# Five edits to a mixer-and-MLP layer: the causal mask as a select, the gate weight moved from v to k, a convolution tap and the first norm's squares on ScalarE, and a broadcast load issued earlier

## The chip, the cores and the metric

The kernel runs on one core of one Trainium2 chip. The metric is the device time of one execution in microseconds (us). The kernel before took 1031.86, 1032.71 and 1033.84 us in three runs (median 1032.71). All arithmetic is on float32 data; most matrix products split each float32 operand into a rounded high part and a remainder and add three products of the parts.

## The reference, cut to what matters

One layer over 1024 tokens (rows) of 1024 channels. The steps that the change touches are these:

```
u = x @ w_in                                   # q, k, v, gates, output gate, pooling columns
qk = silu(causal_conv(u[q,k columns], w_conv)) # 4 taps: y[t] = sum_j w[j] * u[t - 3 + j]
# mLSTM, 4 heads x 128, chunk by chunk, with exponential input gate e and decay
C_loc = einsum(e, v, k);  n_loc = einsum(e, k) # state update of a chunk, weighted by e
C = s_old * C + s_new * C_loc
Dlog = where(causal, a_t - a_s + i_s, -inf)    # decay inside a chunk
P = exp(Dlog - m_t);  qk = (q k^T) * P         # masked weights
h = (qk @ v + s_inter * (C q)) / denominator   # then a norm per head and an output gate
mix = concat(h, pooled) @ w_out
x1 = layer_norm(2**0.25 * x + mix, ln1_g, ln1_b)
out = layer_norm(2**0.25 * x1 + square(relu(x1 @ w_ff1)) @ w_ff2, ln2_g, ln2_b)
```

## The kernel before

**Stages.** The tokens are worked on in two halves of 512, each as four tiles of 128 rows. Calls near line 990 lay out the order: projections of the first half (output gate, pooling, v and gates, q, k), then those of the second half with the first half's mLSTM chunks mixed in, then the output projection with the second half's chunks mixed in, and then the MLP. The mLSTM works in chunks of 128 rows, four chunks in each half. The MLP is computed as products over blocks of 512 with seven instead of eight block products per group (a Strassen-like scheme), `jobs` in the code: `n` counts the products, and each has its operands made by `prep`, its 192 matrix instructions by `product`, and its results added into buffers by `evict1` or `evict2`.

**How the order is set.** A list `tasks` holds steps that fall due a number of ticks later (`later`, `tick`); a tick comes twice in a group of projection products. `mlstm` hands each chunk's four stages to it, so that a chunk's small products lie between the large ones. Beyond that the compiler's planner orders each engine's queue: it takes instructions in program order as their inputs come free by its own estimates of their durations, and adds the waits. Each engine and each DMA-issuing queue then runs strictly in that order; an instruction that waits holds back all behind it. `after(...)` keeps one instruction behind another in that plan.

**A chunk** (`mlstm_stages`, line 554). Its decay rows come by SP from a DRAM bounce buffer to `ng` (broadcast over 128 partitions, 128x512) and, but for the first chunk, `si`. GpSimd adds the tile `mask` (0 or -1e30) to `ng` (line 564); ScalarE takes four exponentials with a per-row bias (line 566). TensorE forms q k (line 571) into a bank of the pool `ps_ml`, VectorE multiplies it into `ng` (line 572), GpSimd multiplies q into `si` (line 574). TensorE transposes k (line 578) into a bank of `ps_tr`, ScalarE copies it out as `kt` (line 580), and GpSimd makes `vs`, v times the gate weight `ep` (line 582). Two products give the chunk's output (lines 591, 592), one the state update (line 599, into a bank of `ps_tr`), which VectorE folds into the state `C` (line 605). Lines 608 to 624 are the norm per head on VectorE: many instructions on 4 columns, each on the one before. `ps_ml` and `ps_tr` have two banks each, so a product waits for the engine that empties the bank two uses earlier. The pooling group's map uses `ps_ml` too (line 437); ScalarE and VectorE empty it (lines 440, 441).

**The convolution** (`proj_qk`, line 377) runs on 16 blocks of 128 channels: ScalarE copies a block's product to `u` behind three carried columns (line 393), VectorE forms the first tap (line 397) and adds three more (line 399), ScalarE applies SiLU.

**The first norm** (`out_proj`, line 670): for each pair of row tiles VectorE adds the scaled x to the product (line 697) and takes statistics of each 512 columns (line 698); after the second column half they are joined (line 701), `ln_rsqrt` uses ScalarE for the root, and ScalarE scales and shifts the rows (line 710). The transposes of line 730 need the result.

**The residual** (`residual`, line 862): its first call loads `ln1_g` to all partitions through GpSimd's DMA queue into `lngb` (line 866); its four later calls multiply it into the rows (VectorE, line 870) and add `ln1_b` by an accumulating DMA (line 871). The loop calls it after products 2 to 6. The same queue carries stores of the token operands (line 852) and the accumulating loads that sum weight blocks (line 815).

Of the kernel before, what the change touches and what calls it, by code (L numbers as in the profile page):

```python
# [9 lines left out]
F32 = mybir.dt.float32  # L10
# [5 lines left out]
P = 128  # L16
# [6 lines left out]
def trunk_layer(ctx: ExitStack, tc: tile.TileContext, x, w_in, b_gate, w_conv, hn_g,  # L23
# [36 lines left out]
    def big(shape, dt=F32, name="b"):  # L60
        return bigp.tile(shape, dt, tag="big", name=nm(name))

    def sml(shape, tag, bufs=2):
        return small.tile(shape, F32, tag=tag, name=nm(tag), bufs=bufs)
# [49 lines left out]
    def tick(n=1):  # L114
        for _ in range(n):
            clock[0] += 1
            while True:
                due = [t for t in tasks if t is not None and t[0] <= clock[0]]
                if not due:
# [12 lines left out]
    tri = const.tile([P, P], F32, name="tri")  # L132
    pool.memset(tri, 1.0)
    pool.affine_select(out=tri, in_=tri, pattern=[[1, P]], compare_op=ALU.is_ge, fill=0.0,
                       base=0, channel_multiplier=-1)
    mask = const.tile([P, P], F32, name="mask")
    pool.memset(mask, 0.0)
    pool.affine_select(out=mask, in_=mask, pattern=[[1, P]], compare_op=ALU.is_ge, fill=NEG,
                       base=0, channel_multiplier=-1)
    rcnt = const.tile([P, 16], F32, name="rcnt")  # L140
    for t in range(16):
# [235 lines left out]
    def proj_qk(hf, which, w=None):  # L377
        w = w or wcols(w_in, (OQ, OK)[which], 512)
        dst = (qT, kT)[which]
        for j in range(TT):  # L380
            c = hf * TT + j
            if hf == 0:
                dst[c] = big([P, 4, P], name="qk")
            else:
                if which == 1:
                    qT["pair", c] = zp.tile([P, 2, 4, P], F32, tag="z", name=nm("qk"))
                dst[c] = qT["pair", c][:, which]
        for cp in (0, 2):
            for cb, ps in zip((cp, cp + 1), chan_mm(hf, w, (cp, cp + 1))):
                b = 4 * which + cb  # L390
                u = big([P, HT + 3], name="u")
                dve.tensor_copy(u[:, 0:3], qkc[:, b, :])
                act.copy(u[:, 3:], ps)
                if hf == 0:
                    dve.tensor_copy(qkc[:, b, :], u[:, HT:HT + 3])
                a = big([P, HT], name="cv")
                dve.tensor_scalar(a, u[:, 0:HT], pcol[:, b:b + 1], None, op0=ALU.mult)
                for j in range(1, 4):
                    dve.scalar_tensor_tensor(a, u[:, j:j + HT], pcol[:, 8 * j + b:8 * j + b + 1], a,
                                             op0=ALU.mult, op1=ALU.add)  # L400
                for j in range(TT):
                    act.activation(dst[hf * TT + j][:, cb, :], a[:, j * P:(j + 1) * P], AF.Silu)
            tick()
        return w
# [149 lines left out]
    def mlstm_stages(c):  # L554
        hf, j = divmod(c, TT)
        g = G[hf]
        last = c == S // P - 1
        ng = big([P, 4, P], name="ng")
        si = big([P, 4, P], name="si") if c else None
        for i, t in ((0, ng), (1, si))[:2 if c else 1]:  # L560
            src = g["dr"][i, 4 * j:4 * j + 4, :]
            sp.dma_start(t.rearrange("p h t -> p (h t)"),
                         src.rearrange("h t -> (h t)").unsqueeze(0).to_broadcast([P, 512]))
        pool.tensor_tensor(ng, ng, mask.unsqueeze(1).to_broadcast([P, 4, P]), ALU.add)
        for h in range(4):
            act.activation(ng[:, h, :], ng[:, h, :], AF.Exp, bias=g["b"][:, 1, 4 * j + h:4 * j + h + 1])
        yield
        q, k, v = qT[c], kT[c], v1[c]
        ps = mlps([P, 4, P])
        for h in range(4):  # L570
            pe.matmul(ps[:, h, :], lhsT=k[:, h, :], rhs=q[:, h, :], start=True, stop=True)
        dve.tensor_tensor(ng, ng, ps, ALU.mult)
        if c:
            pool.tensor_tensor(si, si, q, ALU.mult)
        if not last:
            pk = trps([P, 4, P])
            for h in range(4):
                pe.transpose(pk[:, h, :], k[:, h, :], ident)
            kt = big([P, 4, P], name="kt")
            act.copy(kt, pk)  # L580
            vs = big([P, 4, 129], name="vs")
            pool.tensor_tensor(vs, v, g["ep"][:, 4 * j:4 * j + 4].unsqueeze(2).to_broadcast([P, 4, 129]),
                               ALU.mult)
        yield
        o = big([P, 4, 129], name="o")
        for hp in range(2):
            po = mlps([P, 2, 129])
            for i in range(2):
                h = 2 * hp + i
                if c:  # L590
                    pe.matmul(po[:, i, :], lhsT=si[:, h, :], rhs=C[:, h, :], start=True, stop=False)
                pe.matmul(po[:, i, :], lhsT=ng[:, h, :], rhs=v[:, h, :], start=(c == 0), stop=True)
            act.copy(o[:, 2 * hp:2 * hp + 2, :], po)
        if not last:
            for hp in range(2):
                pcl = trps([P, 2, 129])
                for i in range(2):
                    h = 2 * hp + i
                    pe.matmul(pcl[:, i, :], lhsT=kt[:, h, :], rhs=vs[:, h, :], start=True, stop=True)
                if c == 0:  # L600
                    dve.tensor_copy(C[:, 2 * hp:2 * hp + 2, :], pcl)
                else:
                    for i in range(2):
                        h = 2 * hp + i
                        dve.scalar_tensor_tensor(C[:, h, :], C[:, h, :],
                                                 g["so"][:, 4 * j + h:4 * j + h + 1], pcl[:, i, :],
                                                 op0=ALU.mult, op1=ALU.add)
        r, st, mv, w = sml([P, 4], "n_r"), sml([P, 4, 6], "n_st"), sml([P, 4, 2], "n_mv"), sml([P, 4], "n_w")
        den = o[:, :, 128]
        dve.scalar_tensor_tensor(r, den, -1.0, den, op0=ALU.mult, op1=ALU.max)  # L610
        dve.tensor_tensor(r, r, g["thr"][:, 4 * j:4 * j + 4], ALU.max)
        dve.reciprocal(r, r)
        for h in range(4):
# [12 lines left out]
        pt = trps([P, 4, P])  # L626
        for h in range(4):
            pe.transpose(pt[:, h, :], y[:, h, :], ident)
        yh, yl = big([P, 4, P], F32R, "ymh"), big([P, 4, P], F32R, "yml")
        split(yh, yl, pt)  # L630
        yTm[c] = (yh, yl)
# [38 lines left out]
    def out_proj(hf, e, gs=None):  # L670
        w = wo[e]
        for cp in (hf * TT, hf * TT + 2):
# [14 lines left out]
            if e == 0:  # L687
                ln1[cp] = (small.tile([P, 2, 2, 6], F32, tag="l1_st", name=nm("l1_st"), bufs=4),
                           sml([P, 2, 2], "l1_mv"))
            st, mv = ln1[cp]  # L690
            for i, ps in enumerate(pss):
                c = cp + i
                if e == 0:
                    zt[c] = zp.tile([P, 2, 512], F32, tag="z", name=nm("z"))
                    for d in range(2):
                        z[c, d] = zt[c][:, d, :]
                dve.scalar_tensor_tensor(z[c, e], xr[:, i, :], ALPHA, ps, op0=ALU.mult, op1=ALU.add)
                dve.bn_stats(st[:, i, e, :], z[c, e])
            if e == 1:
                for i in range(2):  # L700
                    dve.bn_aggr(mv[:, i, :], st[:, i])
                r = ln_rsqrt(mv[:, :, 1], 2)
                for i in range(2):
                    zs, rs = zt[cp + i], r[:, i:i + 1]
                    if hf == 1 and cp % TT == 2 and i == 1:
                        dve.tensor_scalar(zs, zs, mv[:, i, 0:1], rs, op0=ALU.subtract, op1=ALU.mult)
                        continue
                    shift = sml([P, 1], "l_sh", 4)
                    dve.scalar_tensor_tensor(shift, mv[:, i, 0:1], -1.0, rs, op0=ALU.mult, op1=ALU.mult)
                    act.activation(zs, zs, AF.Identity, scale=rs, bias=shift)  # L710
                    if hf == 0:
                        for d in range(2):
# [309 lines left out]
    for n, (r, ph, i) in enumerate(jobs):  # L1022
# [28 lines left out]
        ends.append(anchor[0])  # L1051
        if ph == 0:
            evict1(i, ps)
            if 2 <= n <= 6:
                residual(n - 2)
        else:
            evict2(i, ps, r)

# [24 lines left out]
```

## Time and profile before

| what | value |
| --- | --- |
| three runs | 1031.86, 1032.71, 1033.84 us |
| the profiled execution | 1032.68 us, of which the span from first to last instruction is 1031.0 us |
| mean granted TensorE clock | 0.993 |
| busy: TensorE matmul, VectorE, ScalarE, GpSimd | 1007.0, 728.5, 453.5, 160.6 us |

The profile page of one execution gives, for each engine, the time in which it was busy; further views group its instructions by code line, list the waits, or show stretches of time. In a row of instructions `out<-in` are the program's names for what is written and read, and a line number is one of the kernel's. PE is TensorE, DVE VectorE, ACT ScalarE, POOL GpSimd, SP the queue that issues most loads. The granted clock (PEclk) is 1.00 at 2.4 GHz and 0.50 at 1.2 GHz.

### The profile page before, as it was taken

The page shows a single profiled execution, that of the slowest core. Times are in us where ns is not written, and L with a number is a line of the kernel's source. Part 1 is how long each engine was busy: PE and PEld are TensorE (multiplying, and loading weights), DVE is VectorE, ACT ScalarE, POOL GpSimd, SP SyncE. Part 2 cuts the span into 40 slices and gives each one's busy share as a digit, 9 for nine tenths or more (in the row PEclk, how much of TensorE's full clock was granted, in tenths as well). Part 3 has the DMA queues.
Part 4 walks back from the last instruction along what each step waited for, and adds up shares of the span by engine and source line. Part 5 has one row for each costly group of instructions (what it writes and reads, how often), then busy time and mean ns, then how long its engine had stood idle before and what let it go on. Part 6 is the DMA issues. An engine that isn't in the chain of part 4 may idle for free.

```text
span 1031.0 us, 12626 instructions
## 1 busy us (share of the span) xinstructions
PE 1007.0 (98%) x4721; PEld 825.6 (80%) x4721; DVE 728.5 (71%) x1199; ACT 453.5 (44%) x649; POOL 160.6 (16%) x199
## 2 busy tenths in 40 slices
PE   9999999999889999999999999999999999999995
PEld 7898789888778887877888888888888888888884
DVE  4664765886988537788875488875488865478877
ACT  4533655648312235443434524434534334534363
POOL 2410002222220103312102002201001302000211
PEclk9999999999989999999999999999999999999998
DMA  8411412423521537997809853809952908902647
GB/s 287 165 62 44 162 43 73 130 75 104 163 62 42 123 129 194 299 290 209 144 2 225 284 183 51 154 1 209 296 178 53 162 1 196 293 1 42 123 92 215
DMA packets 64158, 143.30 MB, mean 139 GB/s; under 512 B 4732, under 2 KB 4832, under 8 KB 64096
## 3 DMA queue, kind: packets, MB, share of 16 engines
q1 hardware_dynamic: 41488, 91.30, 26.5%
q0 software_dynamic: 22368, 50.89, 25.0%
q8 instruction: 37, 0.61, 0.2%
q10 hardware_dynamic: 240, 0.30, 0.1%
q14 instruction: 25, 0.20, 0.1%
HBM read 128.28 MB, written 11.57 MB: 136 GB/s over the span
## 4 chain that ended last, share of the span: by engine, by line
PE 85%; DVE 7%; DMA 3%; issue 2%; ACT 2%; POOL 1%; SPq 0%; DVEq 0%; POOLq 0%; ACTq 0%
PE mm L103 18%; PE mm L104 18%; PE mm L105 18%; PE ml L104 5%; PE ml L103 5%; PE ml L105 5%; PE tr L103 5%; PE tr L104 4%; PE tr L105 4%; DMA w<-in_w_ff_dram 1%; DVE wlo L77 1%; DVE ol L77 1%; PE tr L730 1%; PE tr L174 1%; DMA raw<-in_w_in_dram 1%
## 5 line engine op out<-in xcount | busy, mean ns | idle before, releaser
L77 DVE TENSOR_TENSOR ol<-w,oh 128x1024 fp32r<-128x1024 f32 x112 | 135.8, 1222 | 94.3 <-ACT oh L76 94.1
L76 ACT CAST oh<-w 128x1024 fp32r<-128x1024 f32 x112 | 116.5, 1047 | 152.7 <-PE mm L104 59.0
L103 PE MATMUL mm<-oh,oh 128*128 128x512 f32 x448 | 176.9, 395 | 1.9 <-DVE h L931 1.6
L104 PE MATMUL mm<-ol,oh 128*128 128x512 f32 x448 | 176.7, 394 | 0.9 <-DVE ol L77 0.9
L105 PE MATMUL mm<-oh,ol 128*128 128x512 f32 x448 | 176.3, 394 | 0.0
L815 POOL DMA_DIRECT2D w<-in_w_ff_dram x64 | 76.7, 1281 | 495.3 <-DVE ol L77 473.3
L103 PEld LDWEIGHTS mm<-oh,oh 128*128 128x128 f32 x448 | 84.2, 188 | 22.9 <-ACT oh L76 2.2
L104 PEld LDWEIGHTS mm<-ol,oh 128*128 128x128 f32 x448 | 84.2, 188 | 20.8 <-DVE ol L77 1.3
L105 PEld LDWEIGHTS mm<-oh,ol 128*128 128x128 f32 x448 | 84.2, 188 | 19.8
L104 PE MATMUL ml<-ol,oh 128*128 128x512 f32 x224 | 88.5, 395 | 0.0
L103 PE MATMUL ml<-oh,oh 128*128 128x512 f32 x224 | 88.5, 395 | 0.0
L103 PE MATMUL tr<-oh,oh 128*128 128x512 f32 x224 | 88.3, 394 | 0.0
L105 PE MATMUL ml<-oh,ol 128*128 128x512 f32 x224 | 88.2, 395 | 0.0
L104 PE MATMUL tr<-ol,oh 128*128 128x512 f32 x224 | 88.2, 394 | 0.0
L105 PE MATMUL tr<-oh,ol 128*128 128x512 f32 x224 | 88.1, 393 | 0.0
L77 DVE TENSOR_TENSOR ol<-xs,oh 128x1024 fp32r<-128x1024 f32 x42 | 51.3, 1224 | 47.2 <-ACT oh L76 47.2
L76 ACT CAST oh<-h 128x1024 fp32r<-128x1024 f32 x40 | 41.8, 1048 | 80.3 <-PE ml L104 24.9
L76 ACT CAST oh<-xs 128x1024 fp32r<-128x1024 f32 x42 | 43.9, 1048 | 62.6 <-PE ml L104 38.8
L77 DVE TENSOR_TENSOR wlo<-raw,whi 128x1024 fp32r<-128x1024 f32 (+1 forms) x40 | 51.6, 1299 | 13.6 <-PE mm L105 6.7
L103 PE MATMUL mm<-xT,whi 128*128 128x512 f32 x144 | 57.5, 400 | 0.1
L104 PE MATMUL mm<-xT,whi 128*128 128x512 f32 x144 | 57.0, 396 | 0.0
L105 PE MATMUL mm<-xT,wlo 128*128 128x512 f32 x144 | 56.8, 397 | 0.0
(293 smaller groups left out, 1989.3 us busy)
## 6 DMA issues: line engine op xcount, KB each, us to landing
w<-in_w_ff_dram POOLq DMA_DIRECT2D x64, 512.0 KB, 7.2
w<-in_w_ff_dram SPq DMA_DIRECT2D x58, 512.0 KB, 7.1
xs<-xs SPq DMA_DIRECT2D x42, 512.0 KB, 5.9
raw<-in_w_in_dram SPq DMA_DIRECT2D x27, 512.0 KB, 4.8
xs<-x POOLq DMA_DIRECT2D x12, 512.0 KB, 5.4
raw<-in_w_in_dram SPq DMA_DIRECT2D x8, 520.0 KB, 4.9
raw<-in_w_out_dram SPq DMA_DIRECT2D x8, 512.0 KB, 3.3
xres<-in_x_dram SPq DMA_DIRECT2D x8, 512.0 KB, 3.3
```

The lines of the kernel that those rows point to most:

```text
L76: cast = act.copy(hi, src)
L77: dve.tensor_tensor(lo, src, hi.bitcast(F32), ALU.subtract)
L103: pe.matmul(ps, lhsT=lh, rhs=rh, start=start, stop=False, skip_group_check=grow)
L104: pe.matmul(ps, lhsT=lh, rhs=rl, start=False, stop=False, skip_group_check=grow)
L105: return pe.matmul(ps, lhsT=ll, rhs=rh, start=False, stop=stop, skip_group_check=grow)
L174: pe.transpose(ps[:, a, b, :], raw[:, b, kc * P:(kc + 1) * P], ident)
L730: t0 = pe.transpose(ps[:, j, :], z[hf * TT + j, kb // 4][:, (kb % 4) * P:(kb % 4 + 1) * P], ident)
L815: pool.dma_start(t, w_source(r, ph, q, p), accum_op=ALU.add)
```

## The change

- The tile `mask` is gone. GpSimd sets the entries of `ng` above the diagonal to -1e30 by a select on the index (`affine_select`), in place, instead of an addition.
- `vs` is gone. k is multiplied by the gate weight as its transposed copy is made: four ScalarE instructions with a per-row scale, one a head, instead of one copy; the state update reads v itself.
- The last convolution tap is formed by ScalarE from the product's bank with a per-channel scale; VectorE adds the other three.
- The first norm, but for the last pair of row tiles: the row sums come as a second output of the addition (line 697's instruction), the squares and their sums from four ScalarE instructions after the second column half, and small VectorE instructions make mean and variance of them.
- The first call of `residual`, which loads `lngb`, comes after product 0 instead of product 2. The later calls stay after products 3 to 6.

```diff
-    mask = const.tile([P, P], F32, name="mask")
-    pool.memset(mask, 0.0)
-    pool.affine_select(out=mask, in_=mask, pattern=[[1, P]], compare_op=ALU.is_ge, fill=NEG,
...
-                dve.tensor_scalar(a, u[:, 0:HT], pcol[:, b:b + 1], None, op0=ALU.mult)
-                for j in range(1, 4):
+                act.activation(a, ps, AF.Copy, scale=pcol[:, 24 + b:25 + b])
+                for j in (2, 1, 0):
                     dve.scalar_tensor_tensor(a, u[:, j:j + HT], pcol[:, 8 * j + b:8 * j + b + 1], a,
...
-        pool.tensor_tensor(ng, ng, mask.unsqueeze(1).to_broadcast([P, 4, P]), ALU.add)
+        pool.affine_select(out=ng, in_=ng, pattern=[[0, 4], [1, P]], compare_op=ALU.is_ge, fill=NEG,
+                           base=0, channel_multiplier=-1)
...
-            act.copy(kt, pk)
-            vs = big([P, 4, 129], name="vs")
-            pool.tensor_tensor(vs, v, g["ep"][:, 4 * j:4 * j + 4].unsqueeze(2).to_broadcast([P, 4, 129]),
-                               ALU.mult)
+            for h in range(4):
+                act.activation(kt[:, h, :], pk[:, h, :], AF.Copy, scale=g["ep"][:, 4 * j + h:4 * j + h + 1])
...
-                    pe.matmul(pcl[:, i, :], lhsT=kt[:, h, :], rhs=vs[:, h, :], start=True, stop=True)
+                    pe.matmul(pcl[:, i, :], lhsT=kt[:, h, :], rhs=v[:, h, :], start=True, stop=True)
...
+            last = hf == 1 and cp % TT == 2
...
-                dve.scalar_tensor_tensor(z[c, e], xr[:, i, :], ALPHA, ps, op0=ALU.mult, op1=ALU.add)
-                dve.bn_stats(st[:, i, e, :], z[c, e])
+                if last:
+                    dve.scalar_tensor_tensor(z[c, e], xr[:, i, :], ALPHA, ps, op0=ALU.mult, op1=ALU.add)
+                    dve.bn_stats(st[:, i, e, :], z[c, e])
+                else:
+                    dve.scalar_tensor_tensor(z[c, e], xr[:, i, :], ALPHA, ps, op0=ALU.mult, op1=ALU.add,
+                                             accum_out=st[:, i, e, 0:1])
...
+                    dve.tensor_tensor(neg, st[:, :, 0, 0], st[:, :, 1, 0], ALU.add)
+                    dve.tensor_scalar(neg, neg, -1.0 / 1024, None, op0=ALU.mult)
+                    for i in range(2):
+                        for d in range(2):
+                            act.activation(big([P, 512], name="sq"), z[cp + i, d], AF.Square,
+                                           bias=neg[:, i:i + 1], accum_out=st[:, i, d, 1:2])
+                    dve.tensor_tensor(var, st[:, :, 0, 1], st[:, :, 1, 1], ALU.add)
+                    dve.tensor_scalar(var, var, 1.0 / 1024, None, op0=ALU.mult)
...
-            if 2 <= n <= 6:
-                residual(n - 2)
+            if n == 0 or 3 <= n <= 6:
+                residual(max(n - 2, 0))
```

## Rows read from the trace of the kernel before

**Rows 1.** The page's first part: busy time of TensorE, its share and instructions.

```profile
PE 1007.0 (98%) x4721; PEld 825.6 (80%) x4721; DVE 728.5 (71%) x1199; ACT 453.5 (44%) x649; POOL 160.6 (16%) x199
```

**Rows 2.** The view of waits, TensorE's: line, released by, total us, times, longest.

```profile
PE tr L578 <- DVE C L605: 4.0, 3, 2.3
PE ml L591 <- DVE ypl L441: 2.3, 1, 2.3
PE mm L103 <- DVE h L931: 1.6, 2, 1.1
...
PE mm L104 <- DVE ol L77: 0.9, 1, 0.9
...
PE mm L103 <- ACT oh L76: 0.4, 1, 0.4
```

**Rows 3.** The view of stretches: busy us per engine, granted clock, DMA share, GB/s.

```profile
240.00:260.00 20.00, 20.00 (x94) 16.18 (x93) 11.49 (x19) 16.56 (x32) 6.24 (x5) 1.00 0.46 138
258.00:284.00 26.00, 22.98 (x129) 19.10 (x128) 25.05 (x59) 9.87 (x18) 7.42 (x8) 1.00 0.50 162
280.00:320.00 40.00, 35.46 (x171) 29.50 (x170) 33.80 (x101) 8.82 (x20) 8.92 (x8) 0.91 0.21 66
430.00:447.00 17.00, 17.00 (x75) 13.79 (x74) 9.36 (x9) 5.56 (x8) 6.46 (x7) 1.00 1.06 288
447.00:466.00 19.00, 16.13 (x67) 12.02 (x66) 18.68 (x21) 9.03 (x10) 0.00 (x0) 1.00 1.06 317
```

**Rows 4.** The timeline, 190 to 298 us: start, duration, engine, line, operation.

```profile
190.80 0.97 DVE L470 SCALAR_TENSOR_TENSOR g_lf<-gt,g_t 128x16 f32<-128x16 f32 x1
...
262.42 0.70 DVE L414 TENSOR_TENSOR ps<-pu 128x526 f32<-128x526 f32 x1
263.16 1.56 DVE L419 TENSOR_TENSOR ps<-ps 128x524 f32<-128x524 f32 x1
...
265.61 1.20 POOL L582 TENSOR_TENSOR vs<-v,g_ep 128x516 f32<-128x516 f32 x1 [1.46 <-DVE ps L427]
265.94 1.42 DVE L432 TENSOR_TENSOR dl<-ps,dh 128x512 fp32r<-128x512 f32 x1
...
280.28 1.68 DVE L419 TENSOR_TENSOR ps<-ps 128x524 f32<-128x524 f32 x1
...
296.95 0.16 DVE L616 TENSOR_TENSOR n_w<-n_mv,n_r 128x4 f32<-128x4 f32 x1
296.97 1.30 POOL L564 TENSOR_TENSOR ng<-ng,mask 128x512 f32<-128x512 f32 x1 [8.01 <-DVE n_mv L615]
297.14 1.14 DVE L617 TENSOR_TENSOR n_w<-n_w,n_r 128x4 f32<-128x4 f32 x1
```

**Rows 5.** Groups by line and shape, GpSimd: count, busy us, mean ns, idle before.

```profile
L564 POOL TENSOR_TENSOR ng<-ng,mask 128x512 f32<-128x512 f32 x8 | 10.6, 1319 | 51.5 <-DMA ng<-bounce 30.9 <-DVE cv L399 12.6 <-DVE n_mv L615 8.0
L582 POOL TENSOR_TENSOR vs<-v,g_ep 128x516 f32<-128x516 f32 x7 | 8.0, 1141 | 17.0 <-PE tr L599 8.0 <-PE ml L592 4.7 <-DVE ps L419 2.6
L138 POOL TENSOR_SCALAR_AFFINE_SELECT mask<-mask 128x128 f32<-128x128 f32 x1 | 0.3, 284 | 0.0
```

**Rows 6.** Groups by line and shape, ScalarE and VectorE.

```profile
L566 ACT ACTIVATE ng<-ng,g_ab 128x128 f32<-128x128 f32 x32 | 10.2, 391 | 3.8 <-POOL ng L564 3.5
L970 ACT ACTIVATE sq<-z,l_sum 128x1024 f32<-128x1024 f32 x8 | 9.2, 1149 | 11.1 <-DVE l_sum L969 11.1
L397 DVE TENSOR_SCALAR cv<-u,pcol 128x512 f32<-128x512 f32 x16 | 7.7, 480 | 4.2 <-ACT u L393 4.2
L440 ACT ACTIVATE yph<-ml,pcol 128x512 fp32r<-128x512 f32 x8 | 5.5, 689 | 14.6 <-DVE n_mv L615 10.3 <-PE ml L105 4.3
L580 ACT COPY kt<-tr 128x512 f32<-128x512 f32 x7 | 4.1, 585 | 4.3 <-PE tr L578 2.6 <-DVE dl L432 1.7
```

**Rows 7.** The timeline, 436 to 447 us, one row of VectorE, one of ScalarE.

```profile
436.33 2.36 DVE L870 TENSOR_TENSOR z<-z,lngb 128x1024 f32<-128x1024 f32 x2 [3.96 <-DMA lngb<-in_ln_g_dram]
...
446.24 1.05 ACT L76 CAST oh<-w 128x1024 fp32r<-128x1024 f32 x1 [1.42 <-DMA w<-in_w_ff_dram]
```

More of the change, by code (lines that the diff above doesn't have):

```diff
@@ L134, in trunk_layer @@
     pool.affine_select(out=tri, in_=tri, pattern=[[1, P]], compare_op=ALU.is_ge, fill=0.0,
-                       base=0, channel_multiplier=-1)
-    mask = const.tile([P, P], F32, name="mask")
-    pool.memset(mask, 0.0)
-    pool.affine_select(out=mask, in_=mask, pattern=[[1, P]], compare_op=ALU.is_ge, fill=NEG,
                        base=0, channel_multiplier=-1)
@@ L696, in out_proj @@
                         z[c, d] = zt[c][:, d, :]
-                dve.scalar_tensor_tensor(z[c, e], xr[:, i, :], ALPHA, ps, op0=ALU.mult, op1=ALU.add)
-                dve.bn_stats(st[:, i, e, :], z[c, e])
-            if e == 1:
-                for i in range(2):
-                    dve.bn_aggr(mv[:, i, :], st[:, i])
-                r = ln_rsqrt(mv[:, :, 1], 2)
+                if last:
[4 more added lines that the diff above has]
+                                             accum_out=st[:, i, e, 0:1])
+            if e == 1:
+                if last:
+                    for i in range(2):
+                        dve.bn_aggr(mv[:, i, :], st[:, i])
+                    var = mv[:, :, 1]
+                else:
+                    neg, var = sml([P, 2], "l1_n"), sml([P, 2], "l1_v")
+                    dve.tensor_tensor(neg, st[:, :, 0, 0], st[:, :, 1, 0], ALU.add)
+                    dve.tensor_scalar(neg, neg, -1.0 / 1024, None, op0=ALU.mult)
+                    for i in range(2):
+                        for d in range(2):
[3 more added lines that the diff above has]
+                    dve.tensor_scalar(var, var, 1.0 / 1024, None, op0=ALU.mult)
+                r = ln_rsqrt(var, 2)
                 for i in range(2):
                     zs, rs = zt[cp + i], r[:, i:i + 1]
-                    if hf == 1 and cp % TT == 2 and i == 1:
+                    if last and i == 1:
                         dve.tensor_scalar(zs, zs, mv[:, i, 0:1], rs, op0=ALU.subtract, op1=ALU.mult)
@@ L708, in out_proj @@
                     shift = sml([P, 1], "l_sh", 4)
-                    dve.scalar_tensor_tensor(shift, mv[:, i, 0:1], -1.0, rs, op0=ALU.mult, op1=ALU.mult)
+                    if last:
+                        dve.scalar_tensor_tensor(shift, mv[:, i, 0:1], -1.0, rs, op0=ALU.mult, op1=ALU.mult)
+                    else:
+                        dve.tensor_tensor(shift, neg[:, i:i + 1], rs, ALU.mult)
                     act.activation(zs, zs, AF.Identity, scale=rs, bias=shift)
```

## The prediction

> **What bounds the kernel now.** The page's busy times come first: TensorE is busy 1007.0 us of a span of 1031.0 [rows 1], so 24.0 us are all that a change off TensorE can give back, and the time lost to a slow clock. The view of waits says where: the waits of [rows 2] sum to 4.0 + 2.3 + 1.6 + 0.9 + 0.4 = 9.2 us. The other 14.8 us lie in smaller waits and mostly at the start and the end, where nothing is edited that has weight. The view of stretches then gives the clock [rows 3]: 280 to 320 was granted 0.91, the other stretches there 1.00. With the two levels 1.00 and 0.50, a mean of 0.91 over 40 us is 7.2 us at 1.2 GHz, in which 3.6 us of work at full clock are lost. TensorE was busy 35.46 of these 40 us; the 4.54 missing are the two waits of 2.3 us [rows 2, 3], and I put half of the loss, 1.8 us, to each. The stretch from 447 to 466, with 2.87 us missing in waits of 1.1 us and less, kept the full clock. So the ceiling of what can be won is 9.2 + 3.6 = 12.8 us.
>
> The timeline says why VectorE is late at those waits. An addition over 526 columns takes 0.70 us, but one over 524 took 1.56 and another 1.68; a subtraction over 512 took 1.42; an instruction on 16 columns took 0.97, and one on 4 columns 1.14, where its neighbour on 4 columns took 0.16 [rows 4]. In the last case GpSimd's mask addition began 0.17 us earlier and ended at 298.27, within 0.02 us of where VectorE's instruction ended [rows 4]. The read is that VectorE's instructions with two inputs in SBUF stand while GpSimd works on SBUF. From 258 to 284 VectorE was busy 25.05 of 26 us [rows 3], so each such stand goes on to what is behind it.
>
> **The change part by part.**
>
> *The product v times gate weight leaves GpSimd.* Seven instructions of 1.14 us [rows 5]. It ran beside the 0.97, the 1.56 and the 1.42 us rows (the row at 265.61 stands for three); their excess is about 0.8, 0.86 and 0.72 us against 0.16 and 0.70 [rows 4]. The state waits (line 578 behind line 605) are one of 2.3 and two of 1.7 together [rows 2], and the first excess stands before one of the two, the other before the second. So the 1.7 us should close. Against it stands k's copy: one instruction of 0.585 us becomes four on 128 columns with a per-row operand; four of line 566's kind occupy 4 x 10.2 / 32 = 1.28 us [rows 6], 0.7 more, and before the second wait the product of line 599 follows the copy at once. I take -1.2 us; the ends are -1.7 and +0.7 (nothing closes and the copy is waited for).
>
> *The mask becomes a select.* No row shows a select over 512 columns. From below it is the 0.284 of the 128-column one, from above four of these, 1.14 us; that is still under the addition's 1.32 [rows 5], so a loss is excluded unless the cost grows faster than the columns. I take 0.65, a little under the middle, since a fixed part is in each 0.284. So VectorE may stand some 0.65 less at each mask. At the long state wait the queue holds two additions, each beside a GpSimd instruction: the row of 1.68 stands for both [rows 4]. The product of q into `si` stays and keeps the second one slow. The wait of 2.3 us shrinks by 0.5 from the select, and by what is left of the 1.6 us that VectorE gains after 262 without `vs`; TensorE itself arrives 0.7 earlier there, so about 0.9 is left. I take -1.4 us, ends 0 and -2.3. What remains, 0.9, is shorter than the 1.1 us that left the clock full [rows 2, 3], so I count the 1.8 us of the first clock loss as won; at the other end it is not. At the wait for line 441 (2.3 us) the same 4-column row is in the way: 1.14 becomes some 0.6, so -0.5, and 1.8 us and the slow clock stay; the other end is -2.3 - 1.8 = -4.1, if the planner, with fewer VectorE instructions ahead, puts the norm's chain earlier.
>
> *The row scale is loaded after product 0.* Before, VectorE stood 3.96 us for it in front of four products of line 870, and ScalarE's cast at 446.24 waited for the weight block that was behind it on GpSimd's DMA queue [rows 7]. The load is 128 x 4 KiB = 0.52 MB; at 288 GB/s, the rate from 430 to 447 [rows 3], 1.8 us of that queue. Taken out of it, the weight block lands some 1.5 us earlier, and the waits of 0.4 and 0.9 [rows 2] go: -1.3. The 1.6 us behind line 931 [rows 2] is VectorE's backlog after that; it moves up with TensorE, and I take 0.1 of it. Together -1.4, ends 0 and -2.9. At its new place the load is queued after product 0, on the same queue ahead of the accumulating loads for product 3 and the stores of line 852; SP isn't passed. Its cover there is that TensorE shows no listed wait between 410 and 447; if that is gone it costs those 1.8 us once.
>
> *A tap on ScalarE.* VectorE loses 16 x 0.48 = 7.7 us, ScalarE gains 16 instructions of line 440's kind (from a bank, per-row scale), 16 x 0.689 = 11.0 us [rows 6]. Twelve of the sixteen blocks lie where TensorE has no listed wait. The last four lie before 260: there ScalarE was busy 16.56 of 20 us and VectorE 11.49 [rows 3], so the relief is where it isn't needed, and 2.8 us come where 3.4 are free. I count 0; if the cover is gone it is the slower rival below.
>
> The Trainium skill, "ScalarE: Activation LUTs", section "Rules for kernel authors", says to use VectorE, not ScalarE, for a plain multiplication; the rows agree per instruction, 0.689 against 0.480 us [rows 6]. By that rule alone the tap would be a loss of 3.3 us of engine time; the sum above goes by where the engines have room.
>
> *The first norm's squares.* Per pair of tiles the last two statistics before the root give way to four squares in a row on 512 columns, each between 0.69 (line 440's width) and 1.15 (line 970, twice the width) [rows 6], so the root comes up to 2.8 to 4.6 us later, three times. The first half's two pairs are read by transposes over 25 us later. The third pair's squares fall, at about 373, among ScalarE's evictions of those transposes, for which TensorE has two banks. I take +0.5, between 0 and 2.3 (two squares that an eviction waits for).
>
> The sum against the profiled execution: -1.2 - 1.4 - 1.8 - 0.5 - 1.4 + 0.5 = -5.8, from 1032.68 (a span of 1031.0 and 1.7 around it) to **1026.9 us**. The median of the runs, 1032.71, is the same within 0.03.
>
> **The rivals.**
>
> *All of it closes.* The planner uses the freed VectorE time before both long waits. Then the line 441 wait and its clock loss go as well: a further 1.8 + 1.8, so 1023.3 us. For it: both waits end on VectorE [rows 2]. Against it: the norm's chain is a string of dependent instructions, and the bank is emptied behind it.
>
> *The select locks as long as the addition.* Then VectorE stands as before at both long waits, the clock still falls, and what is left is the DMA term and 0.5 us of `vs`: -1.9, 1030.8 us. For it: only 128 columns of a select have been seen. Against it: the 0.284 row.
>
> The Trainium skill, "SBUF — State Buffer", section "Who interferes with whom", says that a VectorE instruction with two SBUF inputs contends with a GpSimd instruction that reads SBUF, which a select in place does. By that rule the select's stand is its duration, not nothing; the trace shows this for additions only (1.14 against 0.16 us), and no row has a select beside VectorE.
>
> *ScalarE becomes the bound before 260; slower.* ScalarE's queue is in order, and what it frees at the end of that stretch (the exponentials of line 566, the pooling copies) is what VectorE starts its full 26 us on. Four taps are 2.8 us and four times a longer k copy another 2.8, together 5.6 us; if the 3.4 free us lie ahead of the taps and not behind them, VectorE starts 5.6 us late. It gets back 1.6 + 0.5; 3.5 us are added to the waits, the lengthened short wait draws a slow clock of its own (1.8), and the other gains are 1.4 + 0.8: +3.1, 1035.8 us. It decides from the point where the delay of the last exponential before 258 exceeds the 2.1 us that VectorE gets back. For it: 16.56 of 20 busy [rows 3]. Against it: SiLU can start earlier when VectorE has only three taps to add.
>
> **How the numbers follow.** Forecast (1024.5 to 1029.5) 0.50; all closes (1020 to 1024.5) 0.17; the select locks (1029.5 to 1032.5) 0.18; ScalarE (1033 to 1037) 0.15. A measurement of this kernel tells 0.2%, 2.1 us, from no change. Faster is below 1030.6: 0.50 + 0.17 + 0.08 of the third = 0.75. Same: the third's other 0.10 and 0.02 of the fourth = 0.12. Slower 0.13. The range is 1021.0 to 1034.0: it leaves out a twentieth below and most of the fourth case above; the forecast's own is 1024.5 to 1029.5.
>
> **What would show it.** In the profile after: no wait of line 578 over 1 us; the granted clock of 280 to 300 at 1.00; no 4-column instruction over 0.9 us beside the select; a select over 512 columns between 0.3 and 1.14 us; no wait of line 870 for `lngb`, and the cast that was at 446.24 without a wait over 0.3 us. Wrong it is if a wait on ScalarE of over 2 us appears near 258 or 380, if the clock still falls twice, or if the planner has moved the state updates behind longer VectorE work.

## The result, and the profile after

The changed kernel takes **1026.8 us** (median of four runs, 1025.8 to 1027.0), beside 1033.3 for the kernel before in the same comparison: a ratio of 0.9943, 95% interval 0.9928 to 0.9959. The forecast was 1026.9. The sum came out, but not every term of it: one of the terms put at zero cost about 4 us, and two waits closed further than forecast.

The page's first part after, answering to [rows 1]: TensorE is busy 3.4 us less in a span that is 6.9 us shorter.

```profile
PE 1003.6 (98%) x4721; PEld 823.4 (80%) x4721; DVE 709.1 (69%) x1189; ACT 472.0 (46%) x708; POOL 146.3 (14%) x190
```

TensorE's waits after, answering to [rows 2] (line 578 is now 575, 591 is 586, 605 is 600, 931 is 946):

```profile
PE mm L103 <- ACT whi L76: 2.3, 1, 2.3
PE mm L103 <- DVE h L946: 1.7, 2, 1.1
PE ml L586 <- issue: 1.6, 1, 1.6
...
PE tr L575 <- DVE C L600: 0.3, 1, 0.3
```

Line 575's three waits, 4.0 us, are one of 0.3. The wait of line 586 is 1.6 instead of 2.3. On top stands a wait that the kernel before did not have: a product of line 103 waits 2.3 us for ScalarE's cast of a weight piece, `whi`.

The stretches after, answering to [rows 3]; the columns are as there.

```profile
105.00:125.00 20.00, 17.71 (x80) 13.63 (x79) 14.87 (x38) 13.32 (x28) 0.00 (x0) 0.91 0.59 186
258.00:284.00 26.00, 26.00 (x147) 22.19 (x146) 23.40 (x59) 12.44 (x27) 4.93 (x4) 1.00 0.49 161
280.00:320.00 40.00, 38.42 (x207) 32.00 (x207) 35.08 (x127) 10.05 (x25) 7.72 (x7) 1.00 0.25 79
```

Between 258 and 284 TensorE has no gap left, and from 280 to 320 the clock is 1.00 throughout, where it was 0.91 before. Between 105 and 125 it is now 0.91: with the levels 2.4 and 1.2 GHz that is 3.6 us at the lower one, right behind the 2.3 us wait, and 20 us x 0.09 = 1.8 us of work at full clock are lost. In the kernel before this stretch stood at 19.89 us busy and 1.00:

```profile
105.00:125.00 20.00, 19.89 (x96) 15.44 (x95) 16.87 (x46) 12.33 (x26) 0.00 (x0) 1.00 0.57 185
```

**Where the new wait comes from.** ScalarE and the product, 105 to 110 us, in the timeline of the kernel before:

```profile
106.24 0.59 ACT L393 COPY u<-mm 128x512 f32<-128x512 f32 x1 [1.79 <-PE mm L105]
106.73 1.05 ACT L76 CAST whi<-raw 128x1024 fp32r<-128x1024 f32 x1
```

and in the timeline after:

```profile
105.58 0.59 ACT L389 COPY u<-mm 128x512 f32<-128x512 f32 x1 [2.09 <-PE mm L105]
106.06 0.69 ACT L393 ACTIVATE cv<-mm,pcol 128x512 f32<-128x512 f32 x1
106.64 0.59 ACT L389 COPY u<-mm 128x512 f32<-128x512 f32 x1
107.11 0.71 ACT L393 ACTIVATE cv<-mm,pcol 128x512 f32<-128x512 f32 x1
107.69 0.67 ACT L76 CAST xT<-tr 128x256 fp32r<-128x256 f32 x2
108.21 1.09 ACT L76 CAST whi<-raw 128x1024 fp32r<-128x1024 f32 x1
...
109.36 0.50 PE L103 MATMUL mm<-xT,whi 128*128 128x512 f32 x1 [2.29 <-ACT whi L76]
```

The cast used to stand second in ScalarE's queue, behind one copy. The planner has put it behind both copies, both taps and two casts of `xT`; ScalarE is in order, and TensorE has nothing else to do. The 0.11 us that TensorE misses in the row of the kernel before is a wait for this same cast, too short for the list of [rows 2]: the cast had no room there, so what is put ahead of it is paid.

**Beside the select.** GpSimd and VectorE, 279 to 284 and 294 to 297 us, after; answers to [rows 4].

```profile
279.26 3.02 POOL L560 TENSOR_SCALAR_AFFINE_SELECT ng<-ng 128x512 f32<-128x512 f32 x1 [10.92 <-DMA ng<-bounce]
282.26 1.73 POOL L571 TENSOR_TENSOR si<-si,qk 128x512 f32<-128x512 f32 x1
...
294.35 0.64 POOL L560 TENSOR_SCALAR_AFFINE_SELECT ng<-ng 128x512 f32<-128x512 f32 x1 [8.56 <-DMA ng<-bounce]
295.79 1.29 POOL L571 TENSOR_TENSOR si<-si,qk 128x512 f32<-128x512 f32 x1 [0.80 <-DVE r_t L542]
```

```profile
279.34 0.70 DVE L410 TENSOR_TENSOR ps<-pu 128x526 f32<-128x526 f32 x1
279.95 1.22 DVE L77 TENSOR_TENSOR wlo<-raw,whi 128x1024 fp32r<-128x1024 f32 x1
...
281.96 0.87 DVE L415 TENSOR_TENSOR ps<-ps 128x520 f32<-128x520 f32 x1
...
283.02 1.51 DVE L423 SCALAR_TENSOR_TENSOR ps<-ps,pu 128x512 f32<-128x512 f32 x1
...
294.44 0.57 DVE L536 TENSOR_SCALAR r_y<-r_y 128x4 int32<-128x4 int32 x1
...
295.84 1.27 DVE L543 TENSOR_TENSOR r_t<-r_t,r_w 128x4 f32<-128x4 f32 x1
```

The select at 294.35 takes 0.64 us (0.65 was forecast), and the 4-column instruction beside it 0.57; another one on 4 columns, beside the addition, took 1.14 [rows 4]. The product `si`, which stays on GpSimd, does what it did: VectorE's instruction on 512 columns beside it takes 1.51 us at 283, where such a one takes 0.69 elsewhere, and one on 4 columns 1.27 at 295.84.

The select's group by line and shape after, answering to [rows 5]:

```profile
L560 POOL TENSOR_SCALAR_AFFINE_SELECT ng<-ng 128x512 f32<-128x512 f32 x8 | 8.7, 1093 | 46.8 <-DMA ng<-bounce 35.3 <-ACT g_ln L461 11.5
```

The select's mean of 1093 ns is drawn up by two of the eight, 3.02 us at 279.26 and 1.88 at 249.75; the other six take 0.64 to 0.66. The tap's mean of 699 ns and the squares' 714 are near the 689 of line 440 that they were priced from [rows 6].

VectorE's four products with `lngb`, answering to [rows 7], no longer wait:

```profile
L885 DVE TENSOR_TENSOR z<-z,lngb 128x1024 f32<-128x1024 f32 x4 | 4.9, 1218 | 0.0
```

### The profile page after: what moved, and what is told of

It reads as the page before. It is cut to its first block, busy times and chain, and to the rows that moved or that the text cites. A ratio compares the mean times of both kernels' runs of the same rounds, so it can differ in the third digit from the quotient of the medians.

```text
span 1024.1 us, 12663 instructions
## 1 busy us (share of the span) xinstructions
PE 1003.6 (98%) x4721; PEld 823.4 (80%) x4721; DVE 709.1 (69%) x1189; ACT 472.0 (46%) x708; POOL 146.3 (14%) x190
## 4 chain that ended last, share of the span: by engine, by line
PE 89%; DVE 5%; DMA 2%; ACT 2%; issue 1%; POOL 0%; DVEq 0%; ACTq 0%; POOLq 0%
PE mm L103 19%; PE mm L104 19%; PE mm L105 19%; PE ml L103 5%; PE ml L104 5%; PE ml L105 5%; PE tr L103 4%; PE tr L104 4%; PE tr L105 4%; DMA w<-in_w_ff_dram 2%; DVE ol L77 1%; PE tr L170 1%; PE ml L587 1%; DVE h L946 1%; PE ml L586 1%
```

## The experiments

Two theories stood against each other. **A:** the gains come from GpSimd's instructions no longer holding VectorE up, and the tap on ScalarE only costs. **B:** the tap is what relieved VectorE, or the order that the planner wrote did it. The kernels ran in three groups, each on one chip with the kernel before between them, whose medians were 1031.6 (the first four experiments below), 1032.1 (the second-half variant, the scaled k alone, the product of v back, the addition back) and 1032.4 us (the other four); ratios are against that. The changed kernel itself ran only in the first group, so across groups the ratios are compared, not the times. The waits quoted are those of one profiled execution each.

### The changed kernel again

> The changed kernel as it is, beside the three variants of the same call. All theories: 1026.8 us, ratio to the kernel before 0.994 (0.993 to 0.996). TensorE's first long gap is again at about 107 us (2.3 us, the first product of the k columns waiting for ScalarE's cast of their first weight piece), with 3.4 us at half clock behind it.

1027.05 us, ratio 0.9956 (0.9943 to 0.9970). The waits at 107 (2.3 us, clock 0.91) and at 300 (1.4) are there again. Between 430 and 466, however, the same program now shows what the kernel before showed:

```profile
PE mm L103 <- DVE h L946: 1.5, 2, 1.0
...
PE mm L104 <- DVE ol L77: 0.8, 1, 0.8
PE mm L103 <- ACT oh L76: 0.6, 1, 0.6
```

That is 2.9 us, against 1.9 in the first profile and 2.9 in the kernel before. So about 1 us there changes from run to run with nothing edited.

### The tap back on VectorE

```
-                act.activation(a, ps, AF.Copy, scale=pcol[:, 24 + b:25 + b])
-                for j in (2, 1, 0):
+                dve.tensor_scalar(a, u[:, 0:HT], pcol[:, b:b + 1], None, op0=ALU.mult)
+                for j in range(1, 4):
```

> The changed kernel with the tap back on VectorE for all eight blocks. Theory A (the tap on ScalarE cost 2.2 us of wait at 107 us and 1.7 us of half clock behind it, and gave nothing elsewhere): the gap at 107 us is under 0.2 us, the others stay, time 3.9 us under the changed kernel, 1022.9 us, ratio to the kernel before 0.990. Rival B (the lighter VectorE is what shortened the waits at 282 and 299 us): the gap at 107 us goes, but a 2.3 us wait with half clock behind it comes back at about 300 us (0.7 + 1.7 us) or at 282 us (2.3 + 1.7 us), time 1025.3 to 1027 us, ratio 0.992 to 0.994. Rival C (the wait at 107 us comes from the weight's DMA and not from ScalarE's queue): the gap stays, 1026.8 us.

The edit moves all sixteen blocks, eight in each half. 1024.27 us, ratio 0.9931 (0.9918 to 0.9943): 2.8 us under the changed kernel beside it. The gap at 107 is gone, so rival C, the weight's DMA, is out; a wait for the state came back at 280, without a slow clock.

```profile
PE tr L575 <- DVE C L600: 1.6, 2, 1.3
```

Theories A and B were half right: 4.1 us gone (2.3 and 1.8 of clock), 1.3 returned, 2.8 left. The tap on ScalarE does relieve VectorE in the middle.

### The tap alone

The kernel before, with the tap on ScalarE and nothing else.

> The kernel before with the tap on ScalarE and nothing else of the change. Theory A: slower than the kernel before by the wait at 107 us and its half clock, +3.9 us, 1037 us, ratio 1.0038; the waits at 268, 282 and 302 us as before. Rival B (the tap is what relieves VectorE in the middle): the wait at 282 us or at 302 us shorter than 1.6 us and its half clock gone, the two nearly cancel: 1031 to 1034 us, ratio 0.998 to 1.001.

1032.26 us, ratio 1.0005 (0.9995 to 1.0015): no difference.

```profile
PE tr L578 <- DVE C L605: 2.5, 2, 2.0
PE mm L103 <- ACT whi L76: 2.3, 1, 2.3
PE ml L591 <- DVE ypl L441: 2.2, 1, 2.2
```

Two stretches of it, the first for the wait of 2.0 us, the second for that of 2.2:

```profile
280.00:300.00 20.00, 18.05 (x95) 14.78 (x94) 19.16 (x39) 5.91 (x16) 8.87 (x8) 1.00 0.43 132
300.00:320.00 20.00, 17.80 (x93) 15.28 (x92) 16.44 (x64) 3.06 (x7) 0.00 (x0) 0.91 0.08 26
```

The state waits fell from 4.0 [rows 2] to 2.5, and one of the two slow clocks went: 1.5 + 1.8 = 3.3 us won, 4.1 paid at 107. The near zero is two effects of that size. Rival B named this.

### The tap back for two of sixteen blocks

The tap stays on ScalarE but for the pair whose taps stand ahead of the late cast (second pair of the q columns, first half).

```
+                vec = hf == 0 and which == 0 and cp == 2
+                if vec:
+                    dve.tensor_scalar(a, u[:, 0:HT], pcol[:, b:b + 1], None, op0=ALU.mult)
+                else:
+                    act.activation(a, ps, AF.Copy, scale=pcol[:, 24 + b:25 + b])
+                for j in (1, 2, 3) if vec else (2, 1, 0):
```

> The changed kernel with the tap back on VectorE for two of the sixteen blocks alone: the second pair of the q columns in the first half, the one whose taps stand ahead of the weight cast in ScalarE's queue. Theory A: gap at 107 us under 0.5 us instead of 2.3 and no half clock behind it, 1022.9 us, ratio to the kernel before 0.990, the same as with all taps back. Theory A with the cast still second in line (in this kernel ScalarE's order has u, u, cast of xT, then the weight cast, where the kernel before has the weight cast between the two u): a gap of 0.5 to 1.2 us stays, no half clock, 1023.4 to 1024.1 us. Rival B (the taps that stay on ScalarE help elsewhere): below the variant with all taps back by 1 us or more. Rival C: no change, 1026.8 us.

1028.34 us, ratio 0.9968 (0.9955 to 0.9980), beside 0.9956 (0.9943 to 0.9970) for the changed kernel: none of the gain that A forecast; that it is slower is not clear of the noise. The first wait is 1.0, as the second line of A said, but two follow it, and the three make 3.7 us:

```profile
PE tr L170 <- issue: 1.9, 1, 1.9
...
PE mm L103 <- ACT whi L76: 1.0, 1, 1.0
PE mm L105 <- DVE wlo L77: 0.8, 1, 0.8
```

Line 170's transposes need a bank that a cast of `xT`, and VectorE's subtraction behind it, empty. ScalarE's queue in this stretch, from the timeline:

```profile
110.61 0.91 ACT L402 ACTIVATE qk<-cv 128x128 f32<-128x128 f32 x4 [1.74 <-DVE cv L399]
111.61 0.37 ACT L76 CAST xT<-tr 128x256 fp32r<-128x256 f32 x1
```

ScalarE stood 1.74 us for VectorE's convolution, with that cast behind it. That the stand is what the transposes waited for is read from these two rows, not tested. Two blocks changed which engine was late, and the order written for the rest did not fit. The profiled execution, 1026.29 us, had no slow clock up to 1000 us (mean granted clock 0.996). Of the twelve runs the six at 0.995 or 0.996 took 1025.9 to 1028.1 us, the six at 0.992 to 0.994 took 1028.6 to 1031.9; where their clock fell no profile shows.

### The tap on ScalarE in the second half only

This is the second-half variant of the text below. The same lines with `vec = hf == 0`.

> The changed kernel with the tap on VectorE in the first half (q and k of it, eight blocks) and on ScalarE only in the second half. The runs so far: the tap on ScalarE puts 2.3 us and 1.7 us of half clock at 107 us, and takes 1.3 us from the wait at 280 us. Theory A (the cost is the first half's, where the weight cast falls behind the taps; the gain is the second half's, where VectorE is the later engine): no gap over 0.3 us at 107 us, none over 0.5 us at 268 to 290 us; 3.9 us under the changed kernel and 1.3 us under the variant with all taps back: 1023 us, ratio to the kernel before 0.991 to 0.992. Rival (the gain at 280 us is made in the first half, whose keys and values the stage at 190 to 280 us uses): the 1.3 us wait at 280 us stays, time that of the variant with all taps back, 1024.3 us, ratio 0.993.

1022.53 us, ratio 0.9907 (0.9893 to 0.9921): theory A's number. Here ScalarE's cast is again second in line, so the first row below has no wait in it beyond what the kernel before had:

```profile
105.00:125.00 20.00, 19.89 (x95) 15.40 (x94) 16.83 (x46) 12.32 (x26) 0.00 (x0) 1.00 0.59 182
185.00:310.00 125.00, 122.46 (x647) 101.85 (x646) 99.69 (x325) 66.88 (x133) 23.19 (x22) 1.00 0.32 101
```

The second row misses 2.5 us of TensorE in 125; the changed kernel's waits there sum to 2.4 (0.5 + 0.3 + 1.6). So the tap's relief is made entirely by the second half's eight blocks, and its whole cost by the first half's.

### The scaled k alone

The kernel before, with k scaled at its copy and `vs` gone, nothing else.

> The kernel before with one edit: k scaled at its copy by four activations, the multiplication of v on GpSimd gone. Theory A (GpSimd's two-input instructions make VectorE's late, and this one stood ahead of the state updates): the waits at 192 and 268 us (1.0 and 0.8 us) shrink to 0.4 us or less, the one at 282 us from 2.3 to at most 1.4 us, and the half clock behind it goes; 1.4 + 0.9 + 1.7 = 4 us less, ratio 0.996. Rival B (the tap and the select carry the gain, or the order written by the planner): the wait at 282 us stays over 2 us with its half clock; at most 1.4 us less, ratio 0.9985 or more.

1028.00 us, ratio 0.9965 (0.9951 to 0.9978): 4 us less, theory A's sum, from partly other terms.

```profile
PE ml L589 <- issue: 2.4, 1, 2.4
PE tr L578 <- DVE C L603: 2.1, 2, 1.7
...
PE tr L597 <- ACT kt L581: 0.5, 1, 0.5
```

The short waits of 1.0 and 0.8 became 0.34 and nothing, but a wait of 0.5 for the k copy stands in the second one's place. The long one is 1.7, not 1.4; its slow clock is gone. The wait behind the pool's line stays, and so does its clock (0.91 from 300 to 320).

### The product of v back

The changed kernel with `vs` on GpSimd and k copied plain.

> The changed kernel with v multiplied on GpSimd again and k copied plain. Theory A: the waits for the state update come back: about 0.6 us at 195 us and 1 to 2.3 us at 282 us, with 1.7 us of half clock if it is over 2 us; 1.5 to 4 us over the changed kernel: 1028.5 to 1031 us, ratio to the kernel before 0.997 to 1.000. Rival B (with the tap off VectorE there is room enough): under 0.5 us more than the changed kernel, ratio 0.995 to 0.996.

1027.98 us, ratio 0.9962 (0.9949 to 0.9976), where the changed kernel had 0.9943 and 0.9956: 0.6 to 2 us more by the ratios, between the two theories, and the intervals overlap. The trace is theory A's: the state wait at 284 is back at 1.9 us, with a clock of 0.91 from 280 to 300.

```profile
PE tr L575 <- DVE C L602: 2.3, 2, 1.9
```

By its waits and clock near 284 it should have cost about 4 us; at 107 it gave some back (see the last section), and the rest I can't place.

### The addition back

The changed kernel with the mask tile and its addition instead of the select.

> The changed kernel with the mask tile and its addition on GpSimd instead of the select. Theory A (the addition delays VectorE's instructions beside it by 0.9 to 1 us and the select by 0.4 us or less): VectorE's convolution tree at 280 us ends about 0.9 us later, the wait at 282 us is 0.5 to 1.5 us, the wait at 300 us 1.5 to 2.2 us; 0.5 to 2 us over the changed kernel, ratio to the kernel before 0.995 to 0.998. Rival B (the select holds VectorE as long as the addition): within 0.3 us of the changed kernel in waits of TensorE between 185 and 310 us.

1029.30 us, ratio 0.9973 (0.9961 to 0.9984): by the ratios 1.8 us over the one measurement of the changed kernel, whose interval overlaps, and 3.1 over the other. Theory A, by the waits:

```profile
PE ml L589 <- issue: 2.1, 1, 2.1
...
PE tr L578 <- DVE C L603: 1.0, 2, 0.6
```

The wait for the state at 282 is 0.6 instead of none, the one behind the pool's line 2.1 instead of 1.6, and with the 2.1 the slow clock of 300 to 320 (0.91) is back.

### The row scale loaded late

The second-half variant with `if 2 <= n <= 6: residual(n - 2)`, as in the kernel before.

> The variant with the tap on ScalarE only in the second half (1022.5 us, ratio to the kernel before 0.991), with the rows' scale loaded where the kernel before loads it. Theory A (its load stood in the DMA queue ahead of what TensorE waits for at 440 to 465 us): the waits there are 2.3 to 2.9 us instead of 1.5 (the kernel before: 0.4 + 0.9 + 1.0 + 0.5); 0.8 to 1.3 us more, 1023.4 to 1023.9 us, ratio 0.992. Rival B (which of these waits appear varies from run to run: the kernel before with the scaled k alone, which loads the scale late, had 1.0 + 0.5 us): waits within 0.3 us, 1022.5 us, ratio 0.991; only VectorE's wait for the scale comes back, off the path.

1022.52 us, ratio 0.9905 (0.9891 to 0.9920): rival B. VectorE waits 3.8 us for `lngb` again and TensorE's waits between 430 and 466 stay 1.1 and 0.5 us.

```profile
L889 DVE TENSOR_TENSOR z<-z,lngb 128x1024 f32<-128x1024 f32 x4 | 4.7, 1220 | 3.8 <-DMA lngb<-in_ln_g_dram 3.8
```

### The norm's statistics back

The second-half variant with `last = True`. As built, it also normalises every second block on VectorE and, in the first half, leaves out the gain and the bias of these blocks.

> The variant with the tap on ScalarE only in the second half, with the first norm's sums by BN_STATS on VectorE in all four pairs. Theory A (VectorE has room at 286 to 293 us for two BN_STATS of 0.69 us, and ScalarE has room for the squares): the wait at 296 us stays within 0.3 us of 1.55 us, time within 0.5 us of 1022.5 us. Rival B (the squares free VectorE for the convolution's and the pool's results at 296 us): that wait is 2.2 us or more, with 1.7 us of half clock behind it; 0.7 to 2.5 us more, 1023.2 to 1025 us.

1023.70 us, ratio 0.9915 (0.9900 to 0.9929). The wait at 296 is 1.6 us, as without it, at full clock: theory A. It is 1.2 us above the kernel with the scale loaded late, with overlapping intervals; its waits between 440 and 457 (0.2 + 0.8 + 1.0 + 0.5) are 0.9 us more than there, and they vary by as much anyway. Since more than the statistics was changed, it shows only that the squares are not what shortened the wait at 296; what they cost or give by themselves stays open.

### The product of v on GpSimd with one input

The second-half variant, k copied plain.

```
+            for h in range(4):
+                pool.tensor_scalar(vs[:, h, :], v[:, h, :], g["ep"][:, 4 * j + h:4 * j + h + 1], None, op0=ALU.mult)
```

> The variant with the tap on ScalarE only in the second half, with v scaled on GpSimd again, but by four instructions with one tensor input and a scalar per partition each, and k copied plain. Theory A (what makes VectorE late is a GpSimd instruction with two tensor inputs): VectorE's instructions beside these four keep their usual durations (0.68 to 0.70 us for 128x512), waits for the state update as in the variant without (0.3 us, none at 268 to 290 us), 1022.5 us or up to 0.5 us more if GpSimd's four take longer than the copies. Rival B (any GpSimd instruction that streams through SBUF makes VectorE late): VectorE's instructions beside them take 1.1 to 1.6 us, a wait of 1 us or more at 282 us; 1024 to 1026 us.

1023.63 us, ratio 0.9911 (0.9895 to 0.9928). The timeline, GpSimd's row first and VectorE's behind it:

```profile
262.65 3.62 POOL L584 TENSOR_SCALAR vs<-v,g_ep 128x129 f32<-128x129 f32 x5 [8.42 <-PE ml L593]
```

```profile
263.33 0.69 DVE L432 TENSOR_TENSOR dl<-ps,dh 128x512 fp32r<-128x512 f32 x1
...
277.80 1.78 DVE L414 TENSOR_TENSOR ps<-pu 128x526 f32<-128x526 f32 x1
```

And `si` on GpSimd:

```profile
276.78 2.25 POOL L575 TENSOR_TENSOR si<-si,qk 128x512 f32<-128x512 f32 x1
```

Beside the four short instructions VectorE's subtraction took 0.69 us, where it took 1.42 beside `vs` in one piece [rows 4]; so far theory A. But a wait of 1.3 us for the state stands at 280 all the same. The rows put it down to `si`: in this kernel's order it meets the addition at 277.80, which took 1.78 us. So the run does not decide between one input and short pieces.

### The product si on VectorE

```
-            pool.tensor_tensor(si, si, q, ALU.mult)
+            dve.tensor_tensor(si, si, q, ALU.mult)
```

> The variant with the tap on ScalarE only in the second half, with the last two-input multiplication of this stage (the scaled queries, seven of them) moved from GpSimd to VectorE. Theory A (beside it two VectorE instructions take 0.87 and 1.51 us instead of 0.69, 1.0 us lost, against 0.69 us that the instruction itself takes on VectorE): the wait at 296 us shrinks from 1.55 us by 0.3 us or a little more, 1022 to 1022.3 us. Rival B (on VectorE the instruction stands in a queue and waits there for its operand's DMA): VectorE shows a wait for the bounce buffer's DMA, the waits at 190 to 300 us grow by 1 us or more, 1023.5 us or more.

1021.42 us, ratio 0.9892 (0.9878 to 0.9907), the fastest version. The wait at 296 shrank from 1.5 to 0.2 us, further than theory A had it:

```profile
PE ml L590 <- DVE ypl L441: 0.2, 1, 0.2
```

Of its 1.3 us, 1.1 show between the medians, 1021.4 and, on the same chip, 1022.5 with the scale loaded late; the intervals of the two ratios overlap, so the wait is the surer reading. VectorE did wait in line 575, 1.8 us for the bounce buffer's DMA and 1.5 for ScalarE, but elsewhere, where TensorE was not behind it. The instruction takes 0.69 us there, against 1.3 to 1.7 on GpSimd, where it lengthens VectorE's instructions beside it.

## Why the prediction was right, and where it was not

Point by point, predicted against the two profiled executions:

- **The three state waits and the first slow clock** (predicted -1.2, -1.4, -1.8): measured -1.4, -2.3 and -1.8. The place and the cause were right, the split was not. The working let `vs` close most of it. `vs` alone took the long wait only from 2.3 to 1.7, the tap alone to 2.0; without one of the three edits 0.6 (no select), 1.3 (no tap) or 1.9 (no scaled k) remain, and none does with all three. The reading that fits is one backlog of VectorE of which each edit takes some.
- **The wait on line 441** (predicted -0.5, slow clock stays): -0.7, and the clock loss of 1.8 us went too. The mechanism, a shorter stand of the norm's chain beside the select, was right: with the addition back the wait is 2.1 and the clock falls; with the tap back it is 1.6 and it does not. The step that failed is "1.8 us and the slow clock stay".
- **The row scale** (predicted -1.4): 1.0 less in the two profiles, but loading it late changes nothing (1022.52 beside 1022.53 us, ratios 0.9905 and 0.9907), and the same program varies between 1.9 and 2.9 us here. The load was hidden behind other work; the step that it delayed a weight block that TensorE waited for is refuted in the second-half variant, and in the changed kernel the cast still waits 1.1 us for its block. The four waits of [rows 2] from one execution were taken for fixed.
- **The tap** (predicted 0): +2.3 of wait and +1.8 of clock at 107, against 1.3 us and more won near 280. The step that failed is "twelve of the sixteen blocks lie where TensorE has no listed wait", which was read as room. In the queue before, TensorE already waited 0.11 us for the cast, too short to be listed: there was no room at all, in an order that the planner rewrites. The slower rival had the mechanism, a ScalarE queue that falls late and draws a slow clock, and looked for it before 260; there ScalarE had room, and the relief, called "where it isn't needed" for the last four blocks, was worth more than nothing for the second half's eight, of which these are four. That the late cast is a matter of order, and not of ScalarE's load, is read from the queue; no run keeps the taps on ScalarE and holds the cast ahead of them.
- **The squares** (predicted +0.5): 0; no wait of TensorE between 310 and 410 us is over 0.2, before or after.
- **What was to show it**: the state waits under 1 us, the clock of 280 to 300, the select's 0.64 us and the 4-column instruction beside it came as named. Two signs failed: two selects took 1.88 and 3.02 us, and ScalarE's casts of weight blocks went on waiting for their DMA. The sign of a wrong prediction, over 2 us of wait on ScalarE, came, but at 107 and not near 258 or 380.

The measured parts sum to -1.4 - 2.3 - 1.8 - 0.7 - 1.8 - 1.0 + 4.1 = -4.9. The two profiled executions differ by 6.9 (1032.7 and 1025.8), the second profile of the changed kernel by 4.7 (1028.0): of the 2 us over, 0.7 lie before 105 us (the first copy of the timelines above starts at 105.58, before at 106.24, in the second profile of the changed kernel at 106.33), which changes from run to run; the rest no row places. So 1026.9 stands on a sum in which 4.1 us of cost were left out, and 2.9 us of gain (0.9 of the long wait, 1.8 of the second clock, 0.2 at line 441). The mechanism was right for the state waits and the select; that the total is right within 0.2 us is partly luck.

The rule of the Trainium skill, "ScalarE: Activation LUTs", "Rules for kernel authors", that a plain multiplication belongs on VectorE, agrees with the first half's blocks (ratio 0.9907 with them on VectorE, 0.9956 on ScalarE) and not with the second half's (0.9907 with them on ScalarE, 0.9931 with all on VectorE). The outcome goes by which engine TensorE waits for next, not by the instruction's own price.

## What to carry to other kernels

Moving work to a less busy engine is priced by what its queue does next, not by its share: look for the instruction behind the moved one that TensorE waits for, and how long before its need it ended. When several edits feed one backlog, split them by runs with one edit alone and one edit missing, since an edit that seems worth nothing can be a gain and a cost of 4 us, which can be had apart (here a ratio of 0.991 instead of 0.996). Before pricing a wait, see whether it, and the slow clock behind it, is there in a second execution of the same program.

## What the runs showed of the hardware

- **Who stands depends on who came first.** The select at 279.26 took 3.02 us, while VectorE's two-input instructions beside it kept 0.70 and 1.22; the addition in its place, in the kernel with the addition back, took 3.80 us in the same way. Only from where GpSimd got in did VectorE's instruction grow: 0.87 us beside the select, 1.53 beside the addition. The Trainium skill, "SBUF — State Buffer", "Who interferes with whom", says that the order of issue decides who is blocked, and counts any GpSimd instruction that reads SBUF; these rows agree. So a select holds VectorE up too, but by 0.2 to 0.4 us in these rows (0.87 against 0.70, 0.57 against 0.17), where `si` adds 0.8 and 1.1.

```profile
279.69 3.80 POOL L564 TENSOR_TENSOR ng<-ng,mask 128x512 f32<-128x512 f32 x1 [10.80 <-DMA ng<-bounce]
```

- **Two inputs are not needed.** The prediction read that VectorE's instructions with two inputs in SBUF stand. The one of 0.57 us beside the select has one input, and so has one on 4 columns that took 1.31 us in the kernel before; GpSimd's `si` ran there from 298.51 for 1.29 us.

```profile
298.52 1.31 DVE L539 TENSOR_SCALAR r_y<-r_w 128x4 int32<-128x4 int32 x1
```

- **Here a slow clock and later waits stood for each other.** Behind the 2.3 us at 107 the changed kernel had a clock of 0.91 from 105 to 125 and 17.71 us busy; with the addition or the product of v back, the clock stayed at 1.00, but TensorE waited 0.3 and 0.8 us more and was busy 16.6. In work at full clock that is 17.71 - 1.8 = 15.9 against 16.6, so the slow clock cost 0.7 us there and not 1.8. These kernels differ in other edits too, so this is a reading of three profiles, not a test.
- **Two gaps of nearly one length, two clocks.** The wait of 2.0 us at 284 with the tap alone left the stretch to 300 at 1.00; that of 1.9 us at 284 with the product of v back had 0.91. The length of a gap by itself does not tell here.
- **A slow clock seen in one profile is not in every run.** In the 23 runs of the kernel before in the first group, on one chip, the mean granted clock lay between 0.990 and 0.996; the seven at 0.995 or above took 1030.3 us in the mean, the other sixteen 1032.3. The kernel with the tap back and the second-half variant, in whose profiles no wait is over 1.6 us, had 0.995 to 0.997 in every run. So the terms of 1.8 us above are what one execution showed.
